# One DMA ring for loads and stores, and sums by row, in a mean-subtract-square kernel

## The chip, the cores and the metric

One core of one Trainium2 chip. Times are device microseconds, medians of several executions; most executions of one kernel agree within 0.3%. All runs told here are in the fast state at a granted clock of 1.0.

Three of the core's engines matter: SP, which does nothing here but issue transfers; VectorE (DVE in the views); and ACT. SP and ACT each have a queue for the transfers they issue, also called a ring here. A transfer *lands* when all of its bytes have arrived.

## The reference

```python
x = np.random.randn(1024, 4096).astype(np.float32)      # axis = -1
mean = np.mean(x, axis=axis, keepdims=True)
return ((x - mean) ** 2).astype(np.float32)
```

16.8 MB come in, 16.8 MB go out, and there is little arithmetic on each element.

## The kernel before

Four tiles of 256 rows (two rows on each of 128 partitions, 4.19 MB), each with its own buffer. SP issues the loads, VectorE sums, ACT squares in place with the negative mean as bias, and ACT's own queue issues the stores.

```python
    for i in range(ntiles):                                  # ntiles = 4, Q = 2
        x_tile = pool.tile([P, Q * D], mybir.dt.float32)
        nc.sync.dma_start(out=x_tile, in_=x_t[i])
        x_tiles.append(x_tile)

    for i in range(ntiles):
        x_tile = x_tiles[i].rearrange("p (q d) -> p q d", q=Q)
        # (cut: neg_sum, neg_mean tiles)
        nc.vector.reduce_sum(out=neg_sum, in_=x_tile, axis=mybir.AxisListType.X, negate=True)
        nc.vector.tensor_scalar_mul(out=neg_mean, in0=neg_sum, scalar1=inv_d)
        for q in range(Q):
            nc.scalar.activation(out=x_tile[:, q, :], in_=x_tile[:, q, :],
                func=mybir.ActivationFunctionType.Square, bias=neg_mean[:, q:q + 1], scale=1.0)
        nc.scalar.dma_start(out=out_t[i], in_=x_tiles[i])
```

Of the kernel before, what the change touches and what calls it, by code (L numbers as in the profile page):

```python
# [2 lines left out]

os.environ.setdefault("NEURON_RT_ULTRASERVER_MODE", "4")

# [4 lines left out]


@with_exitstack
def kernel(
    ctx: ExitStack,
    tc: tile.TileContext,
    x: bass.AP,
    axis: bass.AP,
    out: bass.AP,
):  # L20
    nc = tc.nc

    B, D = x.shape
    P = nc.NUM_PARTITIONS
    Q = 2
    assert B % (P * Q) == 0
    ntiles = B // (P * Q)

    inv_d = 1.0 / float(D)

    x_t = x.rearrange("(n p q) d -> n p (q d)", p=P, q=Q)
    out_t = out.rearrange("(n p q) d -> n p (q d)", p=P, q=Q)

    pool = ctx.enter_context(tc.tile_pool(name="io", bufs=ntiles))
    stats = ctx.enter_context(tc.tile_pool(name="stats", bufs=ntiles))

    x_tiles = []
    for i in range(ntiles):
        x_tile = pool.tile([P, Q * D], mybir.dt.float32)
        nc.sync.dma_start(out=x_tile, in_=x_t[i])  # L40
        x_tiles.append(x_tile)

    for i in range(ntiles):
        x_tile = x_tiles[i].rearrange("p (q d) -> p q d", q=Q)
        neg_sum = stats.tile([P, Q], mybir.dt.float32)
        neg_mean = stats.tile([P, Q], mybir.dt.float32)
        nc.vector.reduce_sum(  # L47
            out=neg_sum,
            in_=x_tile,
            axis=mybir.AxisListType.X,  # L50
            negate=True,
        )
        nc.vector.tensor_scalar_mul(out=neg_mean, in0=neg_sum, scalar1=inv_d)  # L53

        for q in range(Q):
            nc.scalar.activation(  # L56
                out=x_tile[:, q, :],
                in_=x_tile[:, q, :],
                func=mybir.ActivationFunctionType.Square,
                bias=neg_mean[:, q:q + 1],  # L60
                scale=1.0,
            )
        nc.scalar.dma_start(out=out_t[i], in_=x_tiles[i])


# [1 line left out]
_INS = ['x', 'axis']  # L67
_OUTS = [((1024, 4096), 'float32')]
#: Inputs that are plain numbers.
_NUMBERS = {'axis': -1}  # L70


# [26 lines left out]
```

## Time and profile before

| | before |
|---|---|
| median | 84.68 us |
| span of the profiled execution | 82.9 us |
| both DMA queues, share of 16 engines | 95.6% |
| VectorE, ACT busy | 43%, 37% |

A group's columns are: line, engine, operation, output and input, count | busy us, mean ns of one | idle before, and what ended it.

```profile
L47 DVE TENSOR_REDUCE neg_sum<-x_tile 128x2 f32<-128x8192 f32 x4 | 34.7, 8686 | 25.6 <-DMA x_tile<-in_x_dram 25.6
L56 ACT ACTIVATE x_tile<-x_tile,neg_mean 128x4096 f32<-128x4096 f32 x8 | 29.2, 3700 | 24.9 <-DVE neg_mean L53 24.9
```

Both engines idle for some 25 us, and what ends it is, in the end, a load.

The chain of waits (start, length, what): these are four of its pieces. The first has no known releaser in this view; by the timeline it is VectorE's wait for the last load.

```profile
41.35 10.89 another core or an unknown queue
...
52.27 8.70 DVE neg_sum L47
...
60.99 0.18 DVE neg_mean L53
...
61.20 0.35 ACT x_tile L56
```

The last tile lands at 52.27, its sum ends at 60.97, ACT starts on it at 61.20.

### The profile page before, as it was taken

The numbers are of one execution on the slowest core, as the hardware profiler recorded it, in microseconds if no ns is written. First come the engines' busy times: TensorE is split into PE (matmuls) and PEld (weight loads), VectorE is DVE, ScalarE is ACT, GpSimd is POOL, SyncE is SP. The second block draws the span as 40 slices with busy tenths as digits, with TensorE's granted clock in tenths as the row PEclk, the third lists the DMA queues.
The fourth block names the chain that finished last, engine by engine and source line by source line (L and its number), as shares of the span: only waits on it lengthen the run. The fifth ranks groups of instructions, "written<-read, shape, count | busy, mean of one in ns | idle before, by whom it ended". The sixth has DMA issues, their size and how long they took to land.

```text
span 82.9 us, 75 instructions
## 1 busy us (share of the span) xinstructions
DVE 35.4 (43%) x8; ACT 30.5 (37%) x9; POOL 0.2 (0%) x4
## 2 busy tenths in 40 slices
DVE  0000007999599995999900000799950000000000
ACT  0000006000399917998099950000049990000000
POOL 0000000000000000000000000000000000000000
DMA  7779997997999899997997999899796996995990
GB/s 190 300 332 443 506 427 332 506 490 316 459 506 411 348 506 285 443 474 316 490 490 332 443 490 427 348 506 474 332 443 285 506 490 269 506 506 253 506 506 0
DMA packets 1153, 33.55 MB, mean 405 GB/s; under 512 B 129, under 2 KB 129, under 8 KB 129
## 3 DMA queue, kind: packets, MB, share of 16 engines
q1 hardware_dynamic: 576, 16.78, 48.6%
q10 hardware_dynamic: 576, 16.78, 47.0%
q14 instruction: 1, 0.00, 0.0%
HBM read 16.78 MB, written 16.78 MB: 405 GB/s over the span
## 4 chain that ended last, share of the span: by engine, by line
DMA 37%; DVE 21%; another core or an unknown queue 13%; ACT 5%; issue 4%; SPq 1%
DMA x_tile<-in_x_dram 37%; DVE neg_sum L47 21%; ACT x_tile L56 5%; SPq L40 1%; DVE neg_mean L53 0%
## 5 line engine op out<-in xcount | busy, mean ns | idle before, releaser
L47 DVE TENSOR_REDUCE neg_sum<-x_tile 128x2 f32<-128x8192 f32 x4 | 34.7, 8686 | 25.6 <-DMA x_tile<-in_x_dram 25.6
L56 ACT ACTIVATE x_tile<-x_tile,neg_mean 128x4096 f32<-128x4096 f32 x8 | 29.2, 3700 | 24.9 <-DVE neg_mean L53 24.9
L56 ACT ACT_TABLE_LOAD x1 | 1.3, 1283 | 13.1 <-DMA x_tile<-in_x_dram 13.1
L53 DVE TENSOR_SCALAR neg_mean<-neg_sum 128x2 f32<-128x2 f32 x4 | 0.7, 170 | 0.1
L80 POOL MEMSET const-bfloat16-1.0<- 128x1 bf16 x1 | 0.1, 102 | 0.0
L80 POOL MEMSET const-uint8-127<- 128x1 uint8 x1 | 0.1, 102 | 0.0
L80 POOL MEMSET const-float32-1.0<- 128x1 f32 x1 | 0.1, 99 | 0.0
L80 POOL MEMSET const-float32-0.0<- 128x1 f32 x1 | 0.1, 98 | 0.2 <-issue 0.2
## 6 DMA issues: line engine op xcount, KB each, us to landing
x_tile<-in_x_dram SPq DMA_DIRECT2D x4, 4096.0 KB, 26.2
out_dram<-x_tile ACTq DMA_DIRECT2D x4, 4096.0 KB, 17.4
```

The costliest lines, as they stand in the source:

```text
L40: nc.sync.dma_start(out=x_tile, in_=x_t[i])
L47: nc.vector.reduce_sum(out=neg_sum, in_=x_tile, axis=mybir.AxisListType.X, negate=True,)
L53: nc.vector.tensor_scalar_mul(out=neg_mean, in0=neg_sum, scalar1=inv_d)
L56: nc.scalar.activation(out=x_tile[:, q, :], in_=x_tile[:, q, :], func=mybir.ActivationFunctionType.Square, bias=neg_mean[:, q:q + 1], scal ...
L80: nc = _bacc.Bacc("TRN2", target_bir_lowering=False, num_devices=1)
```

## The change

Its intent is to keep all transfers in one ring, first every load, then every store, so that loads come in at full rate and stores follow as a block; and to sum and square row by row, so that a tile is ready earlier. The core of the diff:

```diff
-        nc.vector.reduce_sum(out=neg_sum, in_=x_tile, ...)          # both rows at once, [P, 2]
-        nc.vector.tensor_scalar_mul(out=neg_mean, in0=neg_sum, scalar1=inv_d)
         for q in range(Q):
+            row = tiles[i][:, q * D:(q + 1) * D]
+            nc.vector.reduce_sum(out=neg_sum, in_=row, ...)         # one row, [P, 1]
+            nc.vector.tensor_scalar_mul(out=neg_mean, in0=neg_sum, scalar1=inv_d)
             nc.scalar.activation(...)                               # unchanged but for names
-        nc.scalar.dma_start(out=out_t[i], in_=x_tiles[i])
+        nc.sync.dma_start(out=out_t[i], in_=tiles[i])
```

More of the change, by code (lines that the diff above doesn't have):

```diff
@@ L10 @@
 from concourse._compat import with_exitstack
+F32 = mybir.dt.float32
 @with_exitstack
@@ L32 @@
     out_t = out.rearrange("(n p q) d -> n p (q d)", p=P, q=Q)
-    pool = ctx.enter_context(tc.tile_pool(name="io", bufs=ntiles))
-    stats = ctx.enter_context(tc.tile_pool(name="stats", bufs=ntiles))
-    x_tiles = []
+    io = ctx.enter_context(tc.tile_pool(name="io", bufs=ntiles))
+    stats = ctx.enter_context(tc.tile_pool(name="stats", bufs=2 * ntiles * Q))
+    tiles = []
     for i in range(ntiles):
-        x_tile = pool.tile([P, Q * D], mybir.dt.float32)
+        x_tile = io.tile([P, Q * D], F32)
         nc.sync.dma_start(out=x_tile, in_=x_t[i])
-        x_tiles.append(x_tile)
+        tiles.append(x_tile)
     for i in range(ntiles):
-        x_tile = x_tiles[i].rearrange("p (q d) -> p q d", q=Q)
-        neg_sum = stats.tile([P, Q], mybir.dt.float32)
-        neg_mean = stats.tile([P, Q], mybir.dt.float32)
-        nc.vector.reduce_sum(
-            out=neg_sum,
-            in_=x_tile,
-            axis=mybir.AxisListType.X,
-            negate=True,
-        )
-        nc.vector.tensor_scalar_mul(out=neg_mean, in0=neg_sum, scalar1=inv_d)
-        for q in range(Q):
+        for q in range(Q):
+            row = tiles[i][:, q * D:(q + 1) * D]
+            neg_sum = stats.tile([P, 1], F32)
+            neg_mean = stats.tile([P, 1], F32)
+            nc.vector.reduce_sum(
+                out=neg_sum, in_=row, axis=mybir.AxisListType.X, negate=True
+            )
+            nc.vector.tensor_scalar_mul(out=neg_mean, in0=neg_sum, scalar1=inv_d)
             nc.scalar.activation(
-                out=x_tile[:, q, :],
-                in_=x_tile[:, q, :],
+                out=row,
+                in_=row,
                 func=mybir.ActivationFunctionType.Square,
-                bias=neg_mean[:, q:q + 1],
+                bias=neg_mean,
                 scale=1.0,
             )
-        nc.scalar.dma_start(out=out_t[i], in_=x_tiles[i])
+        nc.sync.dma_start(out=out_t[i], in_=tiles[i])
 _INS = ['x', 'axis']
```

## The prediction

> **What bounds the kernel now.** I read the page's summary first: which engine is busy for the whole span. Neither compute engine is; the DMA row is.
>
> ```profile
> span 82.9 us, 75 instructions
> DVE 35.4 (43%) x8; ACT 30.5 (37%) x9; POOL 0.2 (0%) x4
> ...
> DMA  7779997997999899997997999899796996995990
> ...
> q1 hardware_dynamic: 576, 16.78, 48.6%
> q10 hardware_dynamic: 576, 16.78, 47.0%
> ```
>
> The two queues (q1: loads, from SP; q10: stores, from ACT) are busy 48.6 + 47.0 = 95.6% of 16 engines' span: 79.3 of 82.9 us. The chain of waits is misleading here: it gives VectorE's sum 21%, but it goes back through the last tile's sum only because the last store waited for it; that the transfers behind it could not have gone sooner is something the chain doesn't weigh. So the next view is the timeline, for when each transfer was issued and landed. A load's landing is the end of VectorE's wait for it.
>
> ```profile
> 13.04 8.69 DVE L47 TENSOR_REDUCE neg_sum<-x_tile 128x2 f32<-128x8192 f32 x1 [13.04 <-DMA x_tile<-in_x_dram]
> ...
> 22.75 8.69 DVE L47 TENSOR_REDUCE neg_sum<-x_tile 128x2 f32<-128x8192 f32 x1 [0.82 <-DMA x_tile<-in_x_dram]
> 29.30 0.38 ACTq L63 DMA_DIRECT2D out_dram<-x_tile  x1
> 31.48 0.17 DVE L53 TENSOR_SCALAR neg_mean<-neg_sum 128x2 f32<-128x2 f32 x1
> 31.68 7.31 ACT L56 ACTIVATE x_tile<-x_tile,neg_mean 128x4096 f32<-128x4096 f32 x2 [2.40 <-DVE neg_mean L53]
> 32.46 8.69 DVE L47 TENSOR_REDUCE neg_sum<-x_tile 128x2 f32<-128x8192 f32 x1 [0.82 <-DMA x_tile<-in_x_dram]
> ...
> 41.40 0.34 ACTq L63 DMA_DIRECT2D out_dram<-x_tile  x1
> 45.00 3.69 ACT L56 ACTIVATE x_tile<-x_tile,neg_mean 128x4096 f32<-128x4096 f32 x1
> 52.27 8.69 DVE L47 TENSOR_REDUCE neg_sum<-x_tile 128x2 f32<-128x8192 f32 x1 [10.92 <-DMA x_tile<-in_x_dram]
> ...
> 61.20 0.34 ACTq L63 DMA_DIRECT2D out_dram<-x_tile  x1
> 64.81 3.69 ACT L56 ACTIVATE x_tile<-x_tile,neg_mean 128x4096 f32<-128x4096 f32 x1
> 68.53 0.34 ACTq L63 DMA_DIRECT2D out_dram<-x_tile  x1
> ```
>
> Loads land at 13.04, 22.75, 32.46 and 52.27. The view of the store's line, taken around one issue at a time, gives 23.7, 21.3, 11.2 and 13.5 us from issue to landing, so the stores land at 53.0, 62.7, 72.4 and 82.0. While only loads are in flight a 4.19 MB tile takes 9.71 us (432 GB/s). While only stores are, it takes 9.7, 9.7 and 9.6. Eight tiles at 9.7 are 77.6 of the 82.9 us. The kernel is a stream of transfers with a fixed pace, and a change is worth only what it adds to or takes from the gaps in that stream.
>
> The gaps: from 32.46 to 53.0, 20.5 us, exactly two tiles land (load 3 and store 0). At the pure pace that is 19.4, so 1.1 us is lost in the stretch where the store queue joins the load queue. To see where, I took the view of the queues in three stretches: 13 to 30 us (loads alone), 30 to 36 (the stores join), 36 to 50 (both).
>
> ```profile
> DMA packets 240, 7.34 MB, mean 432 GB/s; under 512 B 16, under 2 KB 16, under 8 KB 16
> ...
> DMA packets 87, 2.33 MB, mean 388 GB/s; under 512 B 16, under 2 KB 16, under 8 KB 16
> ...
> DMA packets 184, 6.03 MB, mean 431 GB/s; under 512 B 0, under 2 KB 0, under 8 KB 0
> ```
>
> Steady mixing costs nothing (431 against 432). The joining costs (432 - 388) / 432 x 6 us = 0.6 us averaged over the engines, and 1.1 us for the engine that lands last. A second gap: store 2 is issued at 61.20, though ACT had finished tile 2 at 45.00 + 3.69 = 48.69; it went out only when the next tile's activation started. By then store 1, landing at 62.7, was all that was left in flight. In the stretch from 61 to 64 us the store queue's share is
>
> ```profile
> q10 hardware_dynamic: 49, 1.08, 84.9%
> ```
>
> so about 0.15 x 3 = 0.45 us of idle engines, averaged. Packets are counted where they start, so this size is rough.
>
> **What the Trainium skill says.** "DMA: Bandwidth & Descriptors", section "Where 436 GB/s comes from", puts the ceiling at 435.2 GB/s for a core's 16 engines; the trace's 432 for a pure stream agrees, and leaves nothing to win beyond the gaps. The same page, "Issuing engines are not separate DMA queues", says that transfers from SP and ACT run on the same 16 engines and interleave: moving the stores to SP buys no bandwidth. Its section "Queues, rings and completion order" says that each engine goes round-robin between the rings it has work for, and takes one ring's descriptors in order. The trace agrees: between 32 and 52 us load 3 and the stores share the engines, and load 3 lands 52.27 - 32.46 = 19.8 us after load 2, twice a tile's time. "VectorE: DVE Perf Modes", section "The perf-mode tier table", gives tensor_reduce no fast mode; 8192 elements in 8.686 us are 1.06 ns each, fixed cost included.
>
> **The change part by part.**
> The stores move to SP's queue. All four loads were issued within 1.89 us from 0.73 us on, and SP then does nothing but wait, so a store goes out as soon as its tile is squared. In the ring it stands behind every load. No byte is added or removed.
>
> Sum and square go by rows. A one-row sum is an estimate from the trace: the page's "The perf-mode tier table" gives one element per cycle and the page's clock is 0.96 GHz, so 8192 take 8.53 us, the fixed part of the measured 8.686 is 0.15, and 4096 take 4.27 + 0.15 = 4.42. With the 0.17 scaling and some 0.03 to hand over, a row is 4.6 and a tile 9.2 us on VectorE, against 8.9 before: 0.3 more per tile, all of it beside transfers, and still under the 9.71 between landings. ACT's eight activations stay 3.70 each. The first row's square overlaps the second row's sum, so a tile is ready about 9.2 + 3.8 = 13.0 us after it lands instead of 16.3 (tile 0: landing 13.04, store issued 29.30). That saves 3.3 us per tile in readiness.
>
> Is readiness on the path? With the loads first and unmixed, tile 3 lands at 32.46 + 9.71 = 42.2 instead of 52.27. The ring then turns to store 0, which has been ready since 13.04 + 13.0 = 26.0: 16 us in hand. Store 1 is ready at 22.75 + 13.0 = 35.8 and reached at 51.9; store 2 at 45.5, reached at 61.5; store 3 at 42.2 + 13.0 = 55.2, reached at 71.2. Every store has 16 us in hand, so the row split is worth nothing by itself (even the old 16.3 us would do), and no gap like the one at 61 us can open.
>
> The sum: the last load lands at 42.2, four stores at 9.67 (the mean of 9.7, 9.7, 9.6) take 38.7, and the last store lands at 80.9 where it landed at 82.0. That is 1.1 us less. The two gaps are not both subtracted in full: the last-landing engine lost its 1.1 us at the joining, and the idle at 61 us was had by engines that were ahead of it. One gap hid the other, so the saving is about 1.1, not 1.1 + 0.45. Against it I set 0.2 us, chosen, not measured, for the turn from load to store inside one ring. 84.68 - 1.1 + 0.2 = 83.8; I put the time at 83.7.
>
> **The rivals.**
> (a) The turn from load to store costs what the joining of the second ring did, 1.1 us, because a first store has to fill an empty pipe. For it: the first load needs 13.04 - 0.73 = 12.3 us to land, 2.6 over the pace. Against: load follows load in that ring at 9.71 with no gap, [...] and a store has 16 us to get there. It would make the time 84.6 to 84.8.
> (b) The loss of overlap hurts: before, compute and stores of early tiles ran beside late loads; now nothing is stored until all is loaded. A reader might expect a serial tail of four stores, 39 us. But the engines are full either way, and before it was three stores deep in the tail already. It would take an engine that isn't full in the load phase to make this matter; 432 GB/s says it is full. If a store did wait for compute, it would show as several us: over 86.
> (c) SP blocks on something: stores are issued in order, and store 0 waits on SP for 23 us after the last load's issue. Nothing stands behind it that is wanted sooner. If the queue took few outstanding transfers, SP would stall, but it took four loads at once, and no more than four are in flight later. Within 0.2 us of the prediction.
> (d) VectorE becomes the bound at 9.2 us a tile. It would need to exceed its 16 us of slack: no effect.
>
> **Range and chances.** The favourable end is the full 1.1 us, and perhaps a little for better-spread engines: 83.2. The other end is rival (a) in full: 84.7. The runs before spread 0.1 us, so noise is small. A gain over 2% needs 1.7 us; the stream's own floor of eight tiles at 9.7, with the start of 13.04 - 9.71 = 3.3 us, lands at 80.9, which leaves nothing to reach that with: 4%. A loss over 2% needs a 1.7 us hole in the stream that the slack makes unlikely: 3%. Within 2%: 93%.
>
> **What would show each step.** Right: all packets on one queue at about 95% or more of 16 engines; loads landing at 13.0, 22.7, 32.5 and 42.2; the second row's sum of the last tile ending near 51.5; stores issued near 26, 36, 45.5 and 55; stores landing some 9.7 apart, the last about 81; eight sums of 4.42 us; the DMA row without a dip near 61 us. Wrong: a dip in the GB/s row at about 42 us means rival (a), and its depth gives its cost; a load that lands later than 42.5 means that stores got among the loads after all; a store issued after its place in the ring was reached means that compute bounds the end; store intervals over 9.8 mean that one ring can't keep the engines fed, which no part of this trace could have told me, since store-only stretches ran from ACT's ring.

## The result, and the profile after

| | before | after |
|---|---|---|
| median (4 runs each) | 84.65 us | 84.25 us |
| lowest to highest | 84.60 to 84.70 | 84.13 to 84.45 |
| ratio of the fast runs, 95% interval | | 0.9957, 0.9938 to 0.9977 |
| span of the profiled execution | 82.9 us | 82.3 us |

Ratios here are the mean time of one kernel's fast runs over that of the other's of the same rounds, so not quite the ratio of the medians. The gain is real and small: 0.4 us where about 1.0 was forecast (84.68 to 83.7).

The page after: busy time, the DMA row and its rate, the single queue.

```profile
span 82.3 us, 86 instructions
...
DVE 35.7 (43%) x16; ACT 30.5 (37%) x9; POOL 0.2 (0%) x4
...
DMA  7679998997997999899979979998998997999890
GB/s 207 287 334 446 509 398 382 493 478 334 462 493 334 446 509 398 382 493 478 287 318 446 509 334 430 509 398 382 493 478 350 446 509 334 430 509 398 382 493 0
...
q1 hardware_dynamic: 1152, 33.55, 96.2%
...
L49 DVE TENSOR_REDUCE neg_sum<-x_tile 128x1 f32<-128x4096 f32 x8 | 35.0, 4415 | 16.0 <-DMA x_tile<-in_x_dram 16.0
```

One queue now holds all packets, and the eight sums take 4.415 us each, as estimated (4.42). The timeline after:

```profile
21.70 0.27 DVE L52 TENSOR_SCALAR neg_mean<-neg_sum 128x1 f32<-128x1 f32 x2
21.88 7.31 ACT L53 ACTIVATE x_tile<-x_tile,neg_mean 128x4096 f32<-128x4096 f32 x2 [7.51 <-DVE neg_mean L52]
...
29.21 30.14 SPq L60 DMA_DIRECT2D out_dram<-x_tile  x4
...
32.46 8.75 DVE L49 TENSOR_REDUCE neg_sum<-x_tile 128x1 f32<-128x4096 f32 x2 [0.79 <-DMA x_tile<-in_x_dram]
...
42.84 8.75 DVE L49 TENSOR_REDUCE neg_sum<-x_tile 128x1 f32<-128x4096 f32 x2 [1.45 <-DMA x_tile<-in_x_dram]
```

Three things are to be seen. First, load 3 lands at 42.84, which is 10.38 us after load 2 and not 9.71. The prediction's sign of rival (a), a dip at about 42 us, is there too: in the two slices from 39.1 to 43.2 us the rate is 287 and 318 GB/s, where the pattern of the row has 334 and 462, or 350 and 446, the other times it comes round. Second, store 0 goes out at 29.21, no earlier than before: the two scalings of a tile run together at 21.70, after both sums, so the order on VectorE is sum, sum, scale, scale, and the first square doesn't overlap the second sum. Third, the dip near 61 us of the kernel before is gone. Taken around one store at a time, issue to landing is 23.3, 23.3, 23.2 and 22.5 us; store 0 lands at 52.5, and store 3, issued at 59.02, at 81.5, three stores in 29.0 us, at the usual 9.7.

### The profile page after: what moved, and what is told of

It reads as the page before. It is cut to its first block, busy times and chain, and to the rows that moved or that the text cites. A ratio compares the mean times of both kernels' runs of the same rounds, so it can differ in the third digit from the quotient of the medians.

```text
span 82.3 us, 86 instructions
## 1 busy us (share of the span) xinstructions
DVE 35.7 (43%) x16; ACT 30.5 (37%) x9; POOL 0.2 (0%) x4
## 4 chain that ended last, share of the span: by engine, by line
DMA 49%; DVE 11%; ACT 5%; ACTq 4%; SPq 1%; issue 0%
DMA x_tile<-in_x_dram 49%; DVE neg_sum L49 11%; ACT x_tile L53 5%; ACTq L91 4%; SPq L41 1%; DVE neg_mean L52 0%
## 5 line engine op out<-in xcount | busy, mean ns | idle before, releaser
L49 DVE TENSOR_REDUCE neg_sum<-x_tile 128x1 f32<-128x4096 f32 x8 | 35.0, 4415 | 16.0 <-DMA x_tile<-in_x_dram 16.0
L52 DVE TENSOR_SCALAR neg_mean<-neg_sum 128x1 f32<-128x1 f32 x8 | 1.1, 149 | 0.0
## 6 DMA issues: line engine op xcount, KB each, us to landing
out_dram<-x_tile SPq DMA_DIRECT2D x4, 4096.0 KB, 23.2
```

What stands on the lines that cost most here:

```text
L49: nc.vector.reduce_sum(out=neg_sum, in_=row, axis=mybir.AxisListType.X, negate=True)
```

## The experiments

Twelve kernels in three calls, each beside the kernel before on the same chip, five rounds. The three calls ran on three chips, so a time is compared across calls by way of the kernel before. The median of before was 84.73, 84.67 and 84.74 in the three calls.

The quantity read in all of them is how long a load takes to land after the one ahead of it: 9.71 us when nothing slows it. A *turn* is a place in the ring where a store follows a load, and the *lead* of a store is the time from its issue to the landing of the load ahead of it. In the diffs, load(i) and store(i) stand for the two DMA calls on SP, kept in program order; `tc.keep_in_program_order` asks the compiler to leave an instruction in its place.

### First call: which part gained, and what the turn costs

**The control** is the changed kernel again.

> The changed kernel again, as the control for the three beside it. Both theories: 84.2 to 84.4 us. The trace should again show the last load landing about 0.6 us late (near 42.8 us) and every store after that 9.7 us apart. If the late landing is chance, it moves or goes in this second trace.

84.30 us (84.28 to 84.32), ratio 0.995. Load 3 lands at 42.99, load 2 at 32.57: 10.42 us, a loss of 0.71. So the late landing is no chance of one trace.

**The queue alone**: the kernel before, its stores on SP, its sum of whole tiles left as it was.

```diff
-        nc.scalar.dma_start(out=out_t[i], in_=x_tiles[i])
+        nc.sync.dma_start(out=out_t[i], in_=x_tiles[i])
```

> Stores on SP's queue, but sum and square as before (one sum per tile). Theory (the queue alone makes the gain): same as the control within 0.1 us, so 84.15 to 84.4. Rival (the row split makes it): no gain, 84.6 to 84.7.

84.29 us (84.08 to 84.53), ratio 0.995. The same as the control: the row split is worth nothing here. Load 3 comes 42.92 - 32.28 = 10.64 us after load 2.

**Two turns in the ring.**

```diff
-        nc.sync.dma_start(out=x_tile, in_=x_t[i])
+        if i < 3:
+            nc.sync.dma_start(out=x_tile, in_=x_t[i])
...
         store(i)
+        if i == 0:
+            load(3)
```

> The changed kernel with the ring in the order load 0, 1, 2, store 0, load 3, store 1, 2, 3: two turns from load to store and one back, where the changed kernel has one turn. Theory (each turn in the ring costs its own refill): each load-to-store turn costs about 0.65 us, the turn back from 0 to 0.65, so 84.9 to 85.6. Rival (only the first store of all pays, as a first use of that direction): as the control, 84.2 to 84.4.

84.55 us (84.47 to 85.18), ratio 0.9997 with an interval of 0.9972 to 1.0021. Neither expectation: 0.25 us over the control, where a loss at each turn would add 0.65 or more. The timeline of this run says where the loss lies:

```profile
22.60 8.74 DVE L50 TENSOR_REDUCE neg_sum<-x_tile 128x1 f32<-128x4096 f32 x2 [0.78 <-DMA x_tile<-in_x_dram]
29.06 0.34 SPq L61 DMA_DIRECT2D out_dram<-x_tile  x1
...
32.31 8.75 DVE L50 TENSOR_REDUCE neg_sum<-x_tile 128x1 f32<-128x4096 f32 x2 [0.78 <-DMA x_tile<-in_x_dram]
38.77 30.59 SPq L61 DMA_DIRECT2D out_dram<-x_tile  x3
...
52.86 8.75 DVE L50 TENSOR_REDUCE neg_sum<-x_tile 128x1 f32<-128x4096 f32 x2 [11.61 <-DMA x_tile<-in_x_dram]
```

Load 2, with store 0 behind it, lands 9.71 us after load 1: that turn cost nothing. Load 3 lands 20.55 us after load 2, with store 0 between them: two tiles are 19.42, so 1.1 is lost there. What differs between the two turns is the lead: store 0 was issued 3.25 us before the load ahead of it landed, store 1 some 14 us before. That gave the theory of the second call.

**The old queues, with ACT in program order.** In the kernel before, the compiled order of ACT has the next tile's first activation ahead of a finished tile's store, for stores 1 and 2. This run undoes only that.

```diff
-            nc.scalar.activation(...)
+            tc.keep_in_program_order(nc.scalar.activation(...))
...
-        nc.scalar.dma_start(out=out_t[i], in_=x_tiles[i])
+        tc.keep_in_program_order(nc.scalar.dma_start(out=out_t[i], in_=x_tiles[i]))
```

> The kernel before with one thing undone: ACT keeps the order of the program, so each store goes out as soon as its tile is squared (store 2 near 48.7 us instead of 61.2), still on ACT's queue and still beside the loads. It closes the gap near 61 us. Prediction's theory (that gap lay in the shadow of the joining, the end is set by the engine that lost 1.1 us there): 84.5 to 84.7. Rival (the gap itself set the end, and closing it is all that the change gained): 84.1 to 84.3.

84.23 us (84.08 to 84.46), ratio 0.9947, 0.993 to 0.9964. The prediction's theory falls and the rival holds. With two rings, and loads and stores mixed as before, all the gain of the change is there. Store 2 now goes out at 48.84, and not at 61.20:

```profile
48.84 0.34 ACTq L63 DMA_DIRECT2D out_dram<-x_tile  x1
51.45 8.69 DVE L47 TENSOR_REDUCE neg_sum<-x_tile 128x2 f32<-128x8192 f32 x1 [9.98 <-DMA x_tile<-in_x_dram]
```

The store queue from 58 to 64 us in the kernel before (packets, MB, share of 16 engines):

```profile
q10 hardware_dynamic: 83, 2.20, 85.4%
```

The same queue and stretch in this run, where it no longer runs dry:

```profile
q10 hardware_dynamic: 94, 2.56, 98.7%
```

The loss where the rings join is still there: load 2 lands at 32.58, store 0 at 29.44 + 23.2 = 52.6, 20.1 us for two tiles, 0.6 over the pace. In the kernel before it was 1.1 by the last engine to land, so one could ask whether a cheaper joining made the gain, and not the closed gap. The trace's packet records speak against it. A 32 KB packet takes 1.21 us on an engine; at the joining load packets that start between 30 and 35 us take longer, up to 2.2 us, and this adds up to 0.68 us for each of the 16 engines in the kernel before and to 0.79 in this run. The joining was no cheaper; the gap is what went. And joining two rings cost about what the turn in one ring does (0.80 us an engine in the control), so changing one for the other gained nothing.

### Second call: the lead of a store

**Store 1 ahead of store 0**, so that the first store in the ring is issued late.

```diff
-        nc.sync.dma_start(out=out_t[i], in_=tiles[i])
+        if i == 1:
+            tc.keep_in_program_order(nc.sync.dma_start(out=out_t[1], in_=tiles[1]))
+            tc.keep_in_program_order(nc.sync.dma_start(out=out_t[0], in_=tiles[0]))
+        elif i > 1:
+            tc.keep_in_program_order(nc.sync.dma_start(out=out_t[i], in_=tiles[i]))
```

> The changed kernel with store 1 ahead of store 0 on SP: the first store is then issued near 38.9 us, about 2.4 us before the ring gets to it, where in the changed kernel store 0 stands in the ring from 29.2 us on. Theory (lead): the last load is slowed only when a store stands behind it long before its turn, as at the second turn of the two-turn run and not at its first, where the store came 2.4 us ahead. So load 3 lands near 42.2 to 42.4 us and the time is 83.4 to 83.7. Rival (the last load before the final stores pays whatever the lead): as the control, load 3 at 42.8 to 43.0, 84.2 to 84.4.

83.49 us (83.45 to 83.58), ratio 0.9857, 0.9843 to 0.987. For a single turn the lead theory holds, and this beats both kernels. Its timeline:

```profile
32.62 8.74 DVE L49 TENSOR_REDUCE neg_sum<-x_tile 128x1 f32<-128x4096 f32 x2 [0.78 <-DMA x_tile<-in_x_dram]
39.08 0.34 SPq L61 DMA_DIRECT2D out_dram<-x_tile  x1
39.47 0.43 SPq L62 DMA_DIRECT2D out_dram<-x_tile  x1
...
42.33 8.74 DVE L49 TENSOR_REDUCE neg_sum<-x_tile 128x1 f32<-128x4096 f32 x2 [0.78 <-DMA x_tile<-in_x_dram]
```

Load 3 lands 9.71 us after load 2, with a store issued 3.25 us before.

**Store 0 unsquared, long ahead** (a wrong result): the two-turn order, with store 0 issued as soon as tile 0 has landed.

```diff
+    store(0)                          # tile 0 as loaded
+    load(3)
-    for i in range(ntiles):
+    for i in range(1, ntiles):
```

> Wrong result on purpose: the two-turn order, but store 0 stores the tile unsquared, so it is issued as soon as load 0 lands, near 13 us, some 18 us before its turn (2.4 us in the two-turn run, where its turn cost nothing). Theory (lead): now the first turn costs about 0.75 us as well; load 2 lands near 33.0 instead of 32.3, and the time is 85.2 to 85.5. Rival (the first of two turns is free by its place): load 2 lands at 32.3 again and the time is that of the two-turn run, 84.5 to 84.7.

84.59 us (84.44 to 84.65), ratio 0.9983. By place, the theory is right: the first turn, free in the two-turn run, now loses. Load 2 lands at 33.52, 10.58 us after load 1 at 22.94, a loss of 0.87. But the time that it gave (85.2 to 85.5) is missed, and the rival's (84.5 to 84.7) met, as the second turn lost nothing: load 3 lands at 52.97, 19.45 us after load 2, though store 1 had a lead of 14 us. A long lead has cost once here, not twice. These 19.45 us take in the turn back from store 0 to load 3 as well, so that one costs nothing here either.

**Store 0 held until tile 1's first row is squared.**

```diff
+            if i == 1 and q == 0:
+                held = tc.keep_in_program_order(nc.sync.dma_start(out=out_t[0], in_=tiles[0]))
+                tc.add_manual_dep(held.ins, act.ins.name, ...)      # wait for that activation
```

> The changed kernel with store 0 held on SP until tile 1's first row is squared, near 35.3 us: 6 us before the ring gets to it. Theory (lead) doesn't say where between 2.4 and 12 us the cost sets in: either as the control (84.2 to 84.4) or as the run with store 1 first (83.4 to 83.7), or between. Rival (lead doesn't matter): as the control.

84.41 us (84.04 to 85.13), ratio 0.9979, wide. Store 0 goes out at 35.28, 6.9 us before load 3 would have landed; load 3 takes 42.95 - 32.42 = 10.53. By the landing, as the control: a lead of 6.9 us is already long.

**Store 1 ahead of store 0, on ACT's own queue.** The edit is that of the first run of this call with `nc.scalar` for `nc.sync` in the stores, and ACT kept in program order.

> Store 1 ahead of store 0, but on ACT's own queue, so that a second ring joins near 39 us, in the last 2.4 us of the loads. Theory (lead, for one ring and for two): few load packets are left for the store's to disturb, so less than the 0.75 us of the joining at 29 us: 83.4 to 84.0. Rival (a second ring's joining costs 0.75 whenever it comes): 84.2 to 84.4.

83.48 us (83.35 to 83.79), ratio 0.9859. Two rings or one: the same, once the first store comes late. Load 3 takes 42.15 - 32.32 = 9.83.

### Third call: how far the theory carries

**Stores in order, store 0 held until all of tile 1 is squared.**

```diff
+        if i == 1:
+            store(0)                  # waits for tile 1's last activation
+        if i > 0:
+            store(i)
```

> The changed kernel with its stores in order 0, 1, 2, 3, but store 0 held until tile 1 is squared (near 39 us). Theory (what counts is the short lead, not that tile 1 goes first): as the run with store 1 first, 83.4 to 83.7, load 3 near 42.3 us. Rival (something about the order of the tiles): 84.2 to 84.4.

83.44 us (83.38 to 83.66), ratio 0.9847, 0.9835 to 0.986. Which tile goes first doesn't matter; when the first store is issued does. Load 3 lands 42.38 - 32.57 = 9.81 us after load 2, with a lead of 3.35 us:

```profile
39.03 0.35 SPq L69 DMA_DIRECT2D out_dram<-x_tile  x1
...
42.38 8.74 DVE L57 TENSOR_REDUCE neg_sum<-x_tile 128x1 f32<-128x4096 f32 x2 [0.88 <-DMA x_tile<-in_x_dram]
```

The view of the queue from 38 to 44 us in the changed kernel:

```profile
DMA packets 81, 2.13 MB, mean 355 GB/s; under 512 B 16, under 2 KB 16, under 8 KB 16
...
q1 hardware_dynamic: 81, 2.13, 95.9%
```

And in this run:

```profile
DMA packets 96, 2.62 MB, mean 437 GB/s; under 512 B 16, under 2 KB 16, under 8 KB 16
```

Same bytes, same ring, same turn. One kernel loses a fifth of the rate for 6 us, as packets are counted at their start; the other doesn't notice the turn. The engines are not idle meanwhile (95.9%): the packets take longer. One by one, in the changed kernel's trace 19 packets take 1.29 to 2.25 us where 1.21 is usual. They are the last packet of load 3 on every engine and the one before it on three; they start between 38.6 and 40.5 us and add up to 0.82 us an engine; the packets of store 0 behind them are at 1.21 again. It is 0.80 in the control and 0.95 with store 0 held to 35.28, from 38.6 us on in both. In this run, whose store comes after that, it is 0.01. Against the kernel before of the same call, the control gained 0.4 us and this run 1.3: issuing a transfer ten microseconds later gained 0.9 us.

**Two turns, both with a short lead**: the two-turn order, with store 1 held until tile 2 is squared.

> The two-turn order with store 1 held until tile 2 is squared, so that both turns from load to store have a lead of about 2.4 us or less. Theory (short lead, no loss, at any turn): the loss of 0.75 us at the second turn goes: 83.6 to 83.9. Rival (one loss per kernel has to come somewhere once there are two turns): 84.5 to 84.7.

84.67 us (84.27 to 85.19), ratio 0.9999. A miss: the time is the rival's (84.5 to 84.7), that one loss has to come somewhere once there are two turns. The first turn is free again (32.41 - 22.69 = 9.72). At the second, store 1 goes out at 48.58, and load 3 lands 20.73 us after load 2, still 1.3 over two tiles. The average engine did gain: its packets lose 0.34 us in all, for 0.94 in the two-turn run. From 44 to 54 us the queue of the two-turn run moved:

```profile
DMA packets 134, 3.87 MB, mean 387 GB/s; under 512 B 16, under 2 KB 16, under 8 KB 16
```

And in this run:

```profile
DMA packets 147, 4.29 MB, mean 429 GB/s; under 512 B 16, under 2 KB 16, under 8 KB 16
```

But the trace's landing times of single engines show one whose part of load 3 landed at 53.1 while half of the engines had theirs by 51.7, and it stayed 1.4 us behind to the end. So the time follows an engine that fell behind, for a reason that stays open, and a short lead isn't a guarantee for turns after the first.

**Three turns, no arithmetic** (a wrong result): every tile is stored as loaded, in the order load 0, 1, store 0, load 2, store 1, load 3, store 2, 3.

> Wrong result on purpose, no arithmetic at all: each tile is stored as loaded, in the ring order load 0, 1, store 0, load 2, store 1, load 3, store 2, 3: three turns from load to store, the stores 9 us and more ahead. In the run with store 0 unsquared the first turn lost 0.84 us and the second, though its store was 12 us ahead, nothing. Theory (the loss is paid once, at the first turn with a long lead): 84.2 to 84.7. Rival (every long lead pays): 85.7 or more.

84.94 us (84.73 to 85.07), ratio 1.0021. Between the two, nearer to the loss that is paid once. Store 0 is issued at 12.82, when load 0 lands, and store 1 at 23.65, when load 1 does: 10.83 us, a loss of 1.1 at the first turn. Load 2 lands at 43.28, 19.63 later, 0.2 over two tiles. The first turn with a long lead pays, the next hardly. And as VectorE and ACT do nothing in this run, neither has a part in the loss.

**Tiles of 128 rows**: `Q = 1`, eight loads and eight stores, packets of 16 KB for 32.

> The changed kernel with tiles of 128 rows in place of 256: eight loads, eight stores, each engine's packets 16 KB instead of 32, one turn with a long lead. If the loss is a share of the packets in work at the turn, it halves, and the time is 83.7 to 84.0. If it is a fixed time, 84.2 to 84.5; twice as many transfers may add up to 0.2 us.

84.53 us (84.44 to 84.67), ratio 0.9979. The loss is halved: the last load comes 43.06 - 37.85 = 5.21 us after the one ahead, against 4.89 for the loads before it, so 0.32 for some 0.7; by the packets it is 0.36 us an engine for 0.80 in the control. The time didn't follow: the first two loads land 0.2 us later than the control's first, a pair of the smaller loads takes 9.78 us instead of 9.71, and a pair of stores 9.72 instead of 9.67, which takes back some 0.6 in all. That the loss goes with the size of the packets in work at the turn fits this one run; transfers were halved with the packets, so it is not shown which of the two counts. Smaller packets are no way to win here.

## Why the prediction was right or wrong

**The bound** (a stream of transfers at 9.7 us a tile, no bytes changed, no effect from the loss of overlap): right. Stores land 9.7 apart after as before, all runs lie within 2% of 84.7, and rivals (b), (c) and (d) made no mark.

**The row split, worth nothing**: right, by the run with the queue alone (84.29 against 84.30). Its working had an error without effect: stores were predicted near 26, 36, 45.5 and 55 us and the first went out at 29.21, as VectorE does both sums before either scaling. The slack of 16 us was 13, and enough.

**One gap hid the other**: this step failed, though its 1.1 us came out right. The prediction took the joining of the second ring (1.1 us on the last engine) for what set the end, and the idle near 61 us for its shadow. The run with ACT in program order closed only the gap and gained 0.5 us, with a joining as dear as before. Why can be worked out from the lines of before: store 2, issued at 61.20, lands 11.2 later and store 3 9.6 after that, at 82.0. Half of the engines had their part of store 1 by 61.8, nearly a microsecond before the slowest, and yet that of store 3 only at 81.9: the gap alone brings the end to there. In the profiled execution the slowest engine of the joining came out at the same 82.0, which hid the gap in that one trace. So 1.1 was the saving whichever of the two was taken for the cause, as the change removes both: luck, as far as the reason goes. The chain of waits, which the prediction set aside as misleading, ran through just this: load 3's landing, the last tile's sum, ACT's start at 61.20.

**The turn from load to store, 0.2 us, chosen**: this term was mis-sized, and it is what the forecast gain was lost to. In the profiled execution the last load landed at 42.84 where 42.2 was forecast, and the last store at 81.5 where 80.9 was. The turn measured 0.67, 0.71 and 0.93 us in three traces of the same ring order (10.38, 10.42 and 10.64 us for 9.71). Rival (a) was nearer with 1.1, but its reason, an empty pipe that a first store has to fill, doesn't hold: a store issued 3.3 us ahead would have to fill it too, and lost 0 to 0.1. The reason against it, that a store has 16 us to get there, was the wrong way round: the time that the first store stands in the ring is what costs. With 3.3 us of lead nothing or 0.1 was lost at a first turn, with 6.9 us already 0.8. The prediction also read a load later than 42.5 as a sign of stores among the loads; in the trace it is the load's own last packets that take longer. A slip besides: its sum gives 83.8, and it put the time at 83.7.

The sum as measured: the joining's loss (0.68 and 0.79 us an engine in two traces) and the turn's (0.80 to 0.91 in three) nearly cancel, and what is left is the gap near 61 us, 0.4 to 0.5 us. The predicted gain of about 1.1 was obtained only when the turn cost next to nothing: 83.44, 83.48 and 83.49 us, 1.2 to 1.3 under before.

**What stays open**: what happens inside a DMA engine when a store waits long behind a load. It is shown that the last packets of the load take longer, with or without compute. In the two runs with a second turn of long lead behind a first one, only the first lost in full. At the joining of two rings load packets are slowed by like amounts, and hardly when the store comes late (0.1 us); that it is the same effect is likely, and not shown. Reading ahead past the turn would fit this; no run here shows it. Nor is it known where between 3.3 and 6.9 us the cost sets in, or why one engine fell behind at the second turn with a short lead. All three kernels with two turns took 84.55 to 84.67 us, so that two turns cost something as such, whatever the leads, is a rival that no run here excludes.

## What to carry to other kernels

In a kernel that is bound by its transfers, look for each store's issue time against the moment its data was ready: a finished tile's store that sits behind the next tile's compute in an engine's order can empty the stream some ten microseconds later, and keeping program order, or moving the store to an idle queue, was worth the same here, 0.4 to 0.5 us. When all loads come first, try holding the first store back until the last load has only a few microseconds to go; here that gained 0.9 us more. And a gap that seems to lie in the shadow of another in one trace should be closed alone before it is written off.

## What the Trainium skill lacked or had wrong

- "DMA: Bandwidth & Descriptors" (sections "Queues, rings and completion order" and "Measured"): nothing on the cost of going from loads to stores. Here the last load before the first store takes 10.4 to 10.8 us for 9.71 when the store is issued some 7 us or more before the load lands, and 9.71 to 9.83 when it is issued 3.3 us before; the load's last packets go from 1.21 to as much as 2.25 us.
- "DMA: Bandwidth & Descriptors", section "Rules for kernel authors", advises to issue a DMA early so as to overlap it with compute. For the first store behind the last load issuing early cost 0.9 us: 84.30 us when issued at 29.3, 83.44 at 39.0 (0.4 and 1.3 under the kernel before of their calls).
- No page says that the compiled order of an engine can put a ready store behind the next tile's activation, 12.5 us (48.69 to 61.20).
